# A depthwise convolution of 31 taps on one Trainium2 core, as three short filters on even and odd tokens

## The chip, the cores and the metric

The kernel runs on one core of one Trainium2 chip. The metric is the device time of one execution in microseconds (us), as the median of several runs. The core has five engines with instruction queues of their own: TensorE (PE in the profile, its weight loads PEld), VectorE (DVE), ScalarE (ACT), GpSimd (POOL) and SyncE (SP), which issues most of the DMAs. Each executes its instructions in the order in which they stand in its queue.

## The reference, cut to what matters

The program is a trunk of two layers over 1024 tokens of 1024 features in float32. In each layer the normed input is multiplied by one matrix `w_in`, and its columns are shared by three token mixers: a convolution module (256 channels), differential attention (6 heads) and a gated DeltaNet (6 heads, forward and backward). Their outputs are concatenated, multiplied by `w_out`, and followed by an MLP with a squared ReLU.

The part that the change touches is the convolution module:

```
def conv_module(u, dw_w, dw_b, ln_w, ln_b):
    a, g = jnp.split(u, 2, axis=-1)
    h = a * jax.nn.sigmoid(g)
    h = depthwise_conv(h, dw_w) + dw_b.astype(h.dtype)   # 31 taps, centred, per channel
    h = layer_norm(h, ln_w, ln_b)
    return jax.nn.silu(h)
```

The part that runs beside it is the preparation of the DeltaNet: for each chunk of 64 tokens and each head a unit lower triangular system is solved. The kernel does that by inverting the triangular matrices.

## The kernel before, in words

Per layer there are three stages that follow each other: the input projections (`w_in_phase`), the attention with the DeltaNet scan woven in, and `w_out` with the MLP. The change lies in the first.

**Input projections.** The normed input lies transposed in SBUF as a high and a low part. Blocks of 128 output columns of `w_in` are computed one after the other, each as three products per 128 x 512 block (`mm3`, L163 to L165). For each block the weights are loaded, split on ACT (L168) and DVE (L169), multiplied on PE, and evacuated with what the block needs. The blocks stand in a list `todo`: two blocks of q, k, v for the DeltaNet, the two halves of the convolution's input (`convin`, 128 channels each), five more DeltaNet blocks, then the blocks for attention (`attqk`) and for v and z. `convin` leaves `u`, 128 channels by 1024 tokens with 15 zeros at each end.

**What is woven in.** Between two blocks the loop advances two generators: `prep` by 8 steps and `conv_module` by 6 steps, as soon as both halves of `u` exist. When the list is down to its last 5 entries, both are drained.

```
while todo and len(todo) > self.LATE:
    todo.pop(0)()
    for _ in range(XN):
        next(prep, None)
    if up[1] is not None:
        for _ in range(CN):
            next(conv, None)
```

**conv_module** (L483) works per half `i` on DVE alone: one instruction for the first tap with the bias (L489), then 30 multiply-adds over 1024 tokens (L491), each with the weight of its tap as a scalar per partition, and each reading and writing the accumulator `ca`. Each is followed by a `yield`. Then, in four quarters, PE transposes `ca`, DVE takes mean and variance, POOL the power for the reciprocal root (L158), and PE transposes back.

**prep** goes over three pairs of heads. `dn_a` transposes keys and queries on PE (L652), squares them on ACT (L654), forms decay products on POOL, DVE and ACT (L682 to L686) and the small products of keys and queries on PE (L696). `invert` then inverts the 64 blocks of 32 x 32 of a pair by substitution on POOL: a loop of 31 steps with two instructions each (L765, L766), each depending on the one before:

```
for j in range(B - 1):
    ...
    nc.gpsimd.tensor_tensor(tv, Lp[...], Xm[...], op=ALU.mult)
    nc.gpsimd.tensor_tensor(Xm[:, j + 1:, 0:w], Xm[:, j + 1:, 0:w], tv, op=ALU.subtract)
    yield
nc.scalar.activation(XT, Xm.rearrange("p a b -> p b a"), AF.Copy)
```

The last line (L768) is the transposed copy on ACT; it reads Xm with a step of 32 elements. Ta and Tt are read back from DRAM, two rounds of small products on PE give the 64 x 64 inverses, and they are stored to `kta` (L804). The inversion of a pair runs beside `dn_a` of the next. The DeltaNet scan that follows loads `kta`.

**What sets the order.** The program is written as one stream. A planner simulates it with a cost for each instruction, takes the ready instruction with the earliest place in the stream (or a raised priority, as for the evacuations of the projections), and writes out one fixed order per engine. On the chip an engine waits at its next instruction, even where a later one could go.

Of the kernel before, what the change touches and what calls it, by code (L numbers as in the profile page):

```python
# [9 lines left out]
F32 = mybir.dt.float32  # L10
# [3 lines left out]
ALU = mybir.AluOpType  # L14
# [4 lines left out]
P = 128  # L19
D = 1024  # L20
S = 1024
# [4 lines left out]
TAPS = 31  # L26
# [52 lines left out]
class K:  # L79
# [403 lines left out]
    def conv_module(self, l, L, W, up, dw, db, lw, lb):  # L483
        nc = self.nc
        cas = []
        for i in range(2):
            ca = W.tile([P, S], F32, tag="ca", bufs=2, name=f"ca{l}_{i}")
            u = up[i]
            nc.vector.tensor_scalar(ca, u[:, 0:S], dw[:, i, 0:1], db[:, i:i + 1], ALU.mult, ALU.add)  # L489
            for k in range(1, TAPS):  # L490
                nc.vector.scalar_tensor_tensor(ca, u[:, k:k + S], dw[:, i, k:k + 1], ca, ALU.mult, ALU.add)  # L491
                yield
            cas.append(ca)
        for q in range(4):
            ps = self.bank("sc0", 1).rearrange("p (t k) -> p t k", k=CONV_CH)
            pa = self.bank("sc1", 1).rearrange("p (i t k) -> p i t k", i=2, k=P)
            xc = W.tile([P, 2, CONV_CH], F32, tag="lnx", bufs=2, name=f"lnx{l}_{q}")
            st = W.tile([P, 2, 6], F32, tag="lnst", bufs=2, name=f"lnst{l}_{q}")
            mv = W.tile([P, 2, 2], F32, tag="lnmv", bufs=2, name=f"lnmv{l}_{q}")
            for tt in range(2):  # L500
                t = 2 * q + tt
                for i in range(2):
                    nc.tensor.transpose(ps[:, tt, i * P:(i + 1) * P], cas[i][:, t * P:(t + 1) * P], self.ident)
                nc.vector.bn_stats(st[:, tt], ps[:, tt])
                nc.vector.bn_aggr(mv[:, tt], st[:, tt])
            r = self.rstd(W, mv[:, :, 1], 1.0, 1e-5, "lnr")
            for tt in range(2):
                nc.vector.tensor_scalar(xc[:, tt], ps[:, tt], mv[:, tt, 0:1], r[:, tt:tt + 1], ALU.subtract, ALU.mult)
            yield
            for i in range(2):  # L510
                for tt in range(2):
                    nc.tensor.transpose(pa[:, i, tt], xc[:, tt, i * P:(i + 1) * P], self.ident)
            yo = W.tile([P, 2, CONV_CH], F32, tag="lnx", bufs=2, name=f"yo{l}_{q}")
            for i in range(2):
                nc.scalar.activation(yo[:, i], pa[:, i].rearrange("p t k -> p (t k)"), AF.Silu, scale=lw[:, i:i + 1], bias=lb[:, i:i + 1])
                nc.scalar.dma_start(self.yd[i, :, q * CONV_CH:(q + 1) * CONV_CH], yo[:, i])
            yield
# [1093 lines left out]
```

## Time and profile before

Three runs gave 2972.13, 2974.86 and 2975.39 us, so a median of 2974.86. The profiled execution took 2969.2 us; its span, from the first instruction to the last, is 2967.3.

| engine | busy us | share of the span | instructions |
|---|---|---|---|
| PE | 2730.7 | 92% | 17292 |
| DVE | 2075.6 | 70% | 3701 |
| ACT | 1405.4 | 47% | 2468 |
| POOL | 868.4 | 29% | 793 |

The share is an average over stages that differ. In the chain of work that ended last, PE has 67% of the span and POOL 11%, of which lines 766 and 765 take 4% and 3%; both belong to the input projections. [...]

### The profile page before, as it was taken

Reading aid. Unit: us, or ns where it says so; the run is one execution under the profiler, and the core shown is the slowest. Engines: PE = TensorE matmul, PEld = TensorE weight load, DVE = VectorE, ACT = ScalarE, POOL = GpSimd, SP = SyncE. Lnnn points to the kernel's source line nnn. Section 1 sums busy time; section 2 is a strip of 40 time slices with the busy share of each in tenths; the row PEclk is TensorE's granted clock in tenths of the full one; section 3 lists DMA queues with packets and bytes.
Section 4 is the critical chain, followed back from the end, with each engine's and each line's share of the span. In section 5 each row is a group of like instructions: output and inputs, shape, how many; then the busy total and the mean of one; then the engine's idle time right before and its main releaser. Section 6 shows DMA issues by size and latency. Waiting matters only on the chain.

```text
span 2967.3 us, 46102 instructions
## 1 busy us (share of the span) xinstructions
PE 2730.7 (92%) x17292; PEld 2189.7 (74%) x17292; DVE 2075.6 (70%) x3701; ACT 1405.4 (47%) x2468; POOL 868.4 (29%) x793
## 2 busy tenths in 40 slices
PE   8987979997999998999999689799879999989997
PEld 7865757766888886888787567577658888868886
DVE  5797317888478776777768772378974877767876
ACT  5432315677346665332554223265863566643334
POOL 2288715747000000000112986276550000000000
PEclk9988979998999999999999889799989999999999
DMA  5557785442325557665446487844332355586553
GB/s 136 153 154 207 209 190 148 130 113 81 122 93 196 208 205 295 236 210 188 152 117 141 124 243 198 212 137 122 100 119 81 110 213 200 195 322 244 204 180 117
DMA packets 415312, 504.73 MB, mean 170 GB/s; under 512 B 125401, under 2 KB 313945, under 8 KB 412786
## 3 DMA queue, kind: packets, MB, share of 16 engines
q1 hardware_dynamic: 359362, 373.92, 42.4%
q10 hardware_dynamic: 55728, 127.88, 11.3%
q8 instruction: 136, 2.23, 0.3%
q14 instruction: 86, 0.70, 0.1%
HBM read 318.01 MB, written 182.12 MB: 169 GB/s over the span
## 4 chain that ended last, share of the span: by engine, by line
PE 67%; POOL 11%; DVE 8%; DMA 8%; issue 3%; ACT 2%; SPq 1%; ACTq 0%; DVEq 0%; POOLq 0%
PE at L163 10%; PE at L164 10%; PE at L165 10%; PE sc L163 4%; PE sc L164 4%; PE sc L165 4%; POOL Xm L766 4%; POOL subt L765 3%; DVE sc L1046 2%; PE at L1044 2%; PE dt L163 2%; PE dt L164 2%; PE dt L165 2%; PE tr L1070 2%; PE dt L861 2%
## 5 line engine op out<-in xcount | busy, mean ns | idle before, releaser
L158 POOL TENSOR_TENSOR pro<-pr,mhalf 128x1 f32<-128x1 f32 x32 | 18.5, 578 | 1415.9 <-DVE pr L207 1413.1
L163 PE MATMUL at<-hTh,wh 128*128 128x512 f32 (+1 forms) x832 | 328.4, 396 | 6.7 <-ACT cp L363 6.7
L165 PE MATMUL at<-hTh,wl 128*128 128x512 f32 (+1 forms) x832 | 326.9, 394 | 6.7 <-DVE wl L169 6.7
L164 PE MATMUL at<-hTl,wh 128*128 128x512 f32 (+1 forms) x832 | 327.2, 393 | 0.0
L1049 ACT ACTIVATE sc<-sc,mx 128x1024 f32<-128x1024 f32 x192 | 220.4, 1149 | 85.2 <-DVE mx L1046 82.8
L165 PEld LDWEIGHTS at<-hTh,wl 128*128 128x128 f32 x832 | 160.8, 193 | 39.6 <-DVE wl L169 8.2
L163 PEld LDWEIGHTS at<-hTh,wh 128*128 128x128 f32 x832 | 161.3, 194 | 38.6 <-ACT cp L363 7.5
L164 PEld LDWEIGHTS at<-hTl,wh 128*128 128x128 f32 x832 | 161.2, 194 | 31.1 <-issue 0.7
L491 DVE SCALAR_TENSOR_TENSOR ca<-cu,dw,ca 128x1024 f32<-128x1024 f32 x120 | 171.3, 1443 | 0.4
L1044 PE MATMUL at<-stk 96*128 96x512 f32 x352 | 146.7, 474 | 18.4 <-DVE mx L1046 17.2
L1046 DVE CUSTOM_DVE_ANT_0 sc<-at,bias,mx 128x512 f32<-128x512 f32 x192 | 142.4, 746 | 24.9 <-PE at L1044 19.3
L1046 DVE CUSTOM_DVE_ANT_0 sc<-at,bias 128x512 f32<-128x512 f32 x192 | 130.1, 684 | 37.1 <-PE at L1044 32.0
L765 POOL TENSOR_TENSOR subt<-Lp,Xm 128x31 f32<-128x31 f32 (+15 forms) x186 | 126.6, 680 | 84.1 <-DMA Lp<-ai 50.9
L1156 ACT ACTIVATE ob<-sb 128x512 fp32r<-128x512 f32 x120 | 74.8, 626 | 156.6 <-PE tr L165 49.3
L766 POOL TENSOR_TENSOR Xm<-Xm,subt 128x31 f32<-128x31 f32 (+15 forms) x186 | 144.8, 778 | 13.0
L163 PE MATMUL at<-ob,oa 128*128 128x512 f32 x356 | 138.3, 391 | 2.1 <-ACT at L1484 2.1
L164 PE MATMUL at<-ob,oa 128*128 128x512 f32 x356 | 138.4, 389 | 0.0
L165 PE MATMUL at<-ob,oa 128*128 128x512 f32 x356 | 138.0, 389 | 0.0
L1070 PE MATMUL tr<-consts,sc 128*128 128x128 f32 x704 | 110.4, 289 | 17.3 <-DVE sc L1066 12.2
L1156 ACT ACTIVATE ob<-w2r 128x512 fp32r<-128x512 f32 x92 | 57.5, 628 | 131.6 <-PE tr L165 48.9
L169 DVE TENSOR_TENSOR wl<-wr,wh 128x1024 fp32r<-128x1024 f32 x48 | 64.9, 1353 | 76.2 <-ACT wh L168 76.2
L1074 ACT ACTIVATE aT<-tr 128x512 f32<-128x512 f32 x160 | 91.7, 592 | 39.0 <-PE tr L1070 38.6
(462 smaller groups left out, 7937.5 us busy)
## 6 DMA issues: line engine op xcount, KB each, us to landing
hd<-oa ACTq DMA_DIRECT2D x120, 512.0 KB, 5.7
oa<-hd SPq DMA_DIRECT2D x120, 512.0 KB, 4.2
w1r<-in_w_ff_dram SPq DMA_DIRECT2D x32, 1024.0 KB, 5.6
w2r<-in_w_ff_dram SPq DMA_DIRECT2D x64, 512.0 KB, 7.0
wr<-in_w_in_dram SPq DMA_DIRECT2D x50, 512.0 KB, 5.0
ld<-hd SPq DMA_DIRECT2D x98, 256.0 KB, 4.1
kta<-kta SPq DMA_DIRECT2D x32, 576.0 KB, 8.5
stk<-qk SPq DMA_DIRECT2D x66, 256.0 KB, 4.8
```

The costliest lines, as they stand in the source:

```text
L163: mm(ps, lhsT=lh, rhs=rh, start=first, stop=False, skip_group_check=more)
L164: mm(ps, lhsT=lh, rhs=rl, start=False, stop=False, skip_group_check=more)
L165: mm(ps, lhsT=ll, rhs=rh, start=False, stop=last, skip_group_check=more)
L491: nc.vector.scalar_tensor_tensor(ca, u[:, k:k + S], dw[:, i, k:k + 1], ca, ALU.mult, ALU.add)
L765: nc.gpsimd.tensor_tensor(tv, Lp[:, j + 1:, j:j + 1].broadcast_to([P, n, w]), Xm[:, j:j + 1, 0:w].broadcast_to([P, n, w]), op=ALU.mult)
L766: nc.gpsimd.tensor_tensor(Xm[:, j + 1:, 0:w], Xm[:, j + 1:, 0:w], tv, op=ALU.subtract)
L1044: mm(ps, lhsT=st[:, 0, t * P:(t + 1) * P], rhs=st[:, 1, ks], start=True, stop=True)
L1046: nc.vector.tensor_tensor_reduce(out=sc[:, ks], in0=ps, in1=self.bias[:, o:o + 512], scale=slope, scalar=mx[:, 0:1] if n2 else 3.0e38, op0 ...
L1049: nc.scalar.activation(sc, sc, AF.Exp, scale=-1.0, bias=mx[:, 1:2], accum_out=oS[:, t, mp:mp + 1])
L1070: nc.tensor.transpose(ps[:, k], pp[0][:, (4 * q + k) * P:(4 * q + k + 1) * P], self.ident)
L1074: nc.scalar.activation(aT[:, 4 * q:4 * q + 4, qi * P:qi * P + P], ps, AF.Copy)
L1156: self.nc.scalar.activation(h, src, AF.Copy)
```

## The change

The 31 taps on all tokens become three filters on the even and the odd samples of `u`. With x_e and x_o the even and odd samples, h0 the 16 taps with even number and h1 the 15 with odd number, the output at odd tokens is y_o = (h0+h1) * x_o + h1 * (x_e shifted - x_o), and at even tokens y_e = (h0+h1) * x_o + h0 * (x_e - x_o). The product with h0+h1 is shared. So per half of the channels there are 16 + 16 + 15 instructions over 512 tokens (the first with the bias), two subtractions that form the differences (one in place in `u`, one into a new tile `x1`), and two small instructions that form h0+h1 in a new tile `hs`. Input and output of each are read and written with a step of two elements. A step of the generator is now two taps, and the forming of the differences is a step of its own: 24 steps for a half in place of 30. The new tiles take 2.2 KB per partition in the same pool.

```diff
-            nc.vector.tensor_scalar(ca, u[:, 0:S], dw[:, i, 0:1], db[:, i:i + 1], ALU.mult, ALU.add)
-            for k in range(1, TAPS):
-                nc.vector.scalar_tensor_tensor(ca, u[:, k:k + S], dw[:, i, k:k + 1], ca, ALU.mult, ALU.add)
-                yield
+
+            H, M = S // 2, S // 2 + 15
+            xe, xo = u[:, 0::2], u[:, 1::2]
+            ye, yo = ca[:, 0::2], ca[:, 1::2]
+            h0, h1 = dw[:, i, 0::2], dw[:, i, 1::2]
+            hs = W.tile([P, 16], F32, tag="hs", bufs=2, name=f"hs{l}_{i}")
+            nc.vector.tensor_tensor(hs[:, 0:15], h0[:, 0:15], h1, op=ALU.add)
+            nc.vector.tensor_copy(hs[:, 15:16], h0[:, 15:16])
+            x1 = W.tile([P, M], F32, tag="x1", bufs=1, name=f"x1_{l}_{i}")
+            nc.vector.tensor_tensor(x1[:, 0:M - 1], xe[:, 1:M], xo[:, 0:M - 1], op=ALU.subtract)
+            nc.vector.tensor_tensor(xe, xe, xo, op=ALU.subtract)
+            yield
+            nc.vector.tensor_scalar(yo, xo[:, 0:H], hs[:, 0:1], db[:, i:i + 1], ALU.mult, ALU.add)
+            for k in range(1, 16):
+                nc.vector.scalar_tensor_tensor(yo, xo[:, k:k + H], hs[:, k:k + 1], yo, ALU.mult, ALU.add)
+                if k % 2:
+                    yield
+            nc.vector.scalar_tensor_tensor(ye, xe[:, 0:H], h0[:, 0:1], yo, ALU.mult, ALU.add)
+            for k in range(1, 16):
+                nc.vector.scalar_tensor_tensor(ye, xe[:, k:k + H], h0[:, k:k + 1], ye, ALU.mult, ALU.add)
+                if k % 2:
+                    yield
+            for k in range(15):
+                nc.vector.scalar_tensor_tensor(yo, x1[:, k:k + H], h1[:, k:k + 1], yo, ALU.mult, ALU.add)
+                if k % 2:
+                    yield
```

## Rows read from the trace of the kernel before

**Rows 1.** Layer 0, busy us (instructions) per engine, clock, DMA.

```profile
150.00:235.00 85.00, 58.71 (x271) 46.37 (x269) 67.78 (x76) 27.95 (x33) 73.66 (x72) 0.82 0.51 135
```

**Rows 2.** PE's waits, whole span: us in total, times, longest.

```profile
PE tr L696 <- ACT sq L654: 36.1, 3, 18.0
```

**Rows 3.** PE timeline, layer 0: start, us, instruction, idle before.

```profile
235.89 1.97 PE L696 MATMUL tr<-kq 64*64 64x128 f32 x18 [17.98 <-ACT sq L654]
```

**Rows 4.** ACT timeline, layer 0: the same columns.

```profile
233.41 1.94 ACT L768 ACTIVATE XT<-Xm 128x1024 f32<-128x1024 f32 x1 [16.65 <-POOL Xm L766]
235.25 0.58 ACT L654 ACTIVATE sq<-tr 128x512 f32<-128x512 f32 x1
```

**Rows 5.** Line 765 on POOL, head pairs 0, 1, 2 of layer 0.

```profile
155.00:234.00 79.00, 23.71 (x31) 0.81 0.47 134
244.00:313.00 69.00, 19.48 (x31) 0.98 0.77 231
323.00:367.00 44.00, 18.56 (x31) 0.96 0.64 183
```

**Rows 6.** Line 766 on POOL in the same stretches.

```profile
155.00:234.00 79.00, 30.90 (x31) 0.81 0.47 134
244.00:313.00 69.00, 25.79 (x31) 0.98 0.77 231
323.00:367.00 44.00, 16.76 (x31) 0.96 0.64 183
```

**Rows 7.** POOL timeline, layer 0: start, us, instruction.

```profile
196.70 2.03 POOL L686 TENSOR_TENSOR De<-De,rho 128x512 f32<-128x512 f32 x1
...
206.99 1.55 POOL L766 TENSOR_TENSOR Xm<-Xm,subt 128x255 f32<-128x255 f32 x1
208.61 1.50 POOL L765 TENSOR_TENSOR subt<-Lp,Xm 128x252 f32<-128x252 f32 x1
...
285.08 1.04 POOL L686 TENSOR_TENSOR De<-De,rho 128x512 f32<-128x512 f32 x1
...
339.52 0.64 POOL L765 TENSOR_TENSOR subt<-Lp,Xm 128x252 f32<-128x252 f32 x1
340.24 0.67 POOL L766 TENSOR_TENSOR Xm<-Xm,subt 128x252 f32<-128x252 f32 x1
```

**Rows 8.** DVE timeline, layer 0; a count stands behind x.

```profile
137.86 6.05 DVE L491 SCALAR_TENSOR_TENSOR ca<-cu,dw,ca 128x1024 f32<-128x1024 f32 x5
...
207.93 1.68 DVE L491 SCALAR_TENSOR_TENSOR ca<-cu,dw,ca 128x1024 f32<-128x1024 f32 x1
...
209.54 1.66 DVE L491 SCALAR_TENSOR_TENSOR ca<-cu,dw,ca 128x1024 f32<-128x1024 f32 x1
...
240.65 0.75 DVE L426 SCALAR_TENSOR_TENSOR qkl<-at,consts,qkh 128x512 fp32r<-128x512 f32 x1
241.31 1.28 DVE L491 SCALAR_TENSOR_TENSOR ca<-cu,dw,ca 128x1024 f32<-128x1024 f32 x1
```

**Rows 9.** DVE groups by line, whole span: busy us, mean ns.

```profile
L491 DVE SCALAR_TENSOR_TENSOR ca<-cu,dw,ca 128x1024 f32<-128x1024 f32 x120 | 171.3, 1443 | 0.4
```

**Rows 10.** ACT groups by line, whole span.

```profile
L168 ACT ACTIVATE wh<-wr 128x1024 fp32r<-128x1024 f32 x50 | 52.9, 1058 | 56.3 <-PE at L164 52.2 <-issue 1.6 <-DMA wr<-in_w_in_dram 1.6
...
L768 ACT ACTIVATE XT<-Xm 128x1024 f32<-128x1024 f32 x6 | 12.1, 2014 | 59.5 <-POOL Xm L766 59.5
```

**Rows 11.** Line 491 on DVE in three stretches of layer 0.

```profile
104.00:137.50 33.50, 17.58 (x12) 1.00 0.43 126
156.00:224.00 68.00, 28.39 (x19) 0.86 0.53 151
244.00:297.00 53.00, 23.11 (x16) 0.97 0.80 234
```

**Rows 12.** Chain of work that ended last, 366 to 440 us.

```profile
373.64 3.87 DMA Ta<-xi
...
396.65 8.02 DMA kta<-kta
```

## The prediction

> **What bounds the kernel now.** I read the busy table first: TensorE (PE) is busy 92% of the span, so the time moves only where PE is left waiting or where the chain runs through something else. The convolution runs only in two stretches, one per layer, so next I asked for the busy time of layer 0's stretch. From 150 to 235 us GpSimd (POOL) is busy 73.66 of 85 us, VectorE (DVE) 67.78, PE only 58.71, and PE's granted clock averages 0.82 [rows 1]. The view of PE's waits says what that hole is: of 36.1 us at line 696 the longest wait is 18.0 [rows 2]; the timeline shows it end at 235.89 [rows 3]. The other half of the 36.1 is its twin in layer 1.
>
> The releaser named there, the square at line 654, is a proxy. In ScalarE's (ACT) timeline that square starts right behind the activation that writes XT (L768), which sat for 16.65 us until POOL's last update of Xm [rows 4]. ACT works in order, so everything PE needs from it stood behind the end of the block inversion on POOL (L765 and L766, 62 dependent instructions per head pair). The end of that loop is what PE waits for.
>
> Then: why is the loop slow? Its last run, for head pair 2, is the measure of an almost undisturbed one: 18.56 + 16.76 = 35.3 us of work. Pair 0 needed 23.71 + 30.90 = 54.6, pair 1 19.48 + 25.79 = 45.3 [rows 5, 6]. POOL's timeline shows how: two steps at 339.52 and 340.24 lie 0.72 us apart, two of about the same size at 206.99 and 208.61 lie 1.6 apart, each instruction itself stretched to 1.5 [rows 7]. The decay products (L686) grow from 1.04 to 2.03 in the same way [rows 7]. In DVE's timeline two taps of the convolution start at 207.93 and 209.54, also 1.61 apart, where five undisturbed ones together take 6.05, 1.20 each [rows 8]. So where both engines have work of this kind they take turns: one DVE instruction, one POOL instruction, and POOL waits about 1.6 - 0.72 = 0.88 us per turn. That wait, not DVE's busy time, is what the convolution costs the critical path.
>
> **The change, part by part.** *Arithmetic on DVE.* Per half of the channels, before: 31 taps at 1.20 start to start [rows 8], the first, which has no second tensor, counted like the others: 37.2 us. With the turns the mean of 120 taps is 1.443 [rows 9]. After: 47 taps on 512 columns, two subtractions of 526 and 527 columns, and two operations on 15 and 1 columns. The row nearest to a 512-column multiply-add with a per-partition factor is L426: one starts at 240.65, the next instruction at 241.31, 0.66 [rows 8]. So 47 x 0.66 = 31.0; the subtractions 2 x 0.66 = 1.3; the small two 0.3 (an estimate: above nothing, at most 0.66 each). Sum 32.6, a saving of 4.6 per half, 18 us over four halves. The saving is that small because half the columns cost 0.66 and not 0.60. I count none of it directly: DVE is not what PE waits for at 235.
>
> [...]
>
> *Stride.* Every operand now takes every second float. No row shows DVE at that stride. Below it, the dense 0.66. Above it, the nearest are ACT's: XT reads Xm 32 floats apart and takes 2014 ns against 1058 for a dense copy of 1024 [rows 10], 1.9 times. I take the dense price, since eight bytes is nearer to dense than to 128, and keep 1.9 as a rival. [...] By ACT's row alone the sum would be the stride rival below.
>
> *POOL's turns.* A tap of half the length keeps POOL waiting 0.54 less (1.20 - 0.66): 0.88 becomes 0.34. There are 47/31 = 1.52 times as many taps to meet. For pair 0 the loop's excess is 54.6 - 35.3 = 19.3, and L686 and L682 inside it some 4 more [rows 5 to 7], 23 us or 26 turns. The convolution has 19 taps in 156 to 224 and 28.39 us of DVE time [rows 11]; the other DVE instructions with two SBUF inputs there (L169, L370, L371, L683) are as many but partly shorter, so I give it 0.6 of the turns (0.5 to 0.8): 16 turns, 14.1 us. After: 16 x 1.52 = 24.3 turns of 0.34, 8.3. Pair 0 ends 5.8 us sooner (3 to 8). Pair 1: 10.0 + 3 = 13 us, 15 turns, 9 of them (16 taps, 23.11 us [rows 11]): 7.9 becomes 4.7, 3.2 sooner. Pair 2 runs when the convolution is over: nothing.
>
> *What PE gets.* The 18.0 us hole shrinks by pair 0's 5.8; ACT and the square have nothing else to wait for. The late part of the stretch hangs on pair 2's end, since Ta lands from 373.64 and the kta transfer starts at 396.65 [rows 12]; between them PE's dense products stand. So the tail moves by between 5.8 and 5.8 + 3.2 = 9.0; I take 7 per layer.
>
> *Start of the loop.* Pair 0 starts when A is stored, behind 12 taps that DVE does from 104 to 137.5 [rows 11]. Each step of the generator issued one tap of 1.20; now it issues two halves, 1.32, after a first step of 1.6 without any tap. For the same 12 steps that is 1.6 + 11 x 1.32 = 16.1 against 12 x 1.20 = 14.4, but fewer columns are then left to do; I cost it at 0.5 per layer (-2 to +3, since the order is found anew).
>
> *Program order.* The two halves need 48 generator steps in place of 60. At six per projection the LayerNorm comes two projections sooner. Its transposes and POOL's rstd move into pair 1's time; they were not late before, so I cost this at nothing. If that cover is gone, it costs POOL four instructions of 0.7 per layer, 3 us.
>
> *Sum.* (7 - 0.5) x 2 = 13 us. The profiled execution takes 2969.2 (span 2967.3 and 1.9 around it), so 2956; the median of the runs is 2974.86, 5.7 above it, so 2962.
>
> **Rivals.** (1) *Nothing arrives (within 6 us).* PE's tail is set by its own dense products and by the loads behind kta, or POOL simply meets a half tap at every step: 62 steps x 0.34 = 21 against 19.3 now. For: DVE is 80% busy there, so more steps can be met [rows 1]. Against: the taps are finite, 19 become 29. Time 2975.
>
> (2) *Stride price, slower.* Place: all 47 taps. At 1.9 times the column time a tap takes 0.12 + 1.9 x 0.54 = 1.15 and 47 of them 54, 17 us more per half. POOL's wait is back at 0.88 - 0.05 with 1.52 times as many turns: 24.3 x 0.83 = 20 against 14.1, and 13.7 x 0.83 = 11.4 against 7.9, 9.5 later per layer; the steps ahead of the loop become 1.6 + 22 x 1.15 = 26.9 and add 12. (9.5 + 12) x 2 = 43: 3018. It decides from where a half tap costs more than about 0.85. Against: eight bytes is far from 128.
>
> (3) *Another order on ACT, either sign.* Each engine's order is written out from a simulated timeline. If one more evacuation that PE needs falls behind pair 1's XT, PE gets a second hole of up to 15 us per layer: 2962 + 30 = 2992. If line 654's square falls ahead of pair 0's XT, the two holes, 36.1 together [rows 2], largely close, and the gain is that and little more: about 2938. Nothing in the profile favours either.
>
> **How the numbers follow.** A measurement of this kernel tells about 0.2%, 6 us, from no change. Chances: forecast 0.45 (2950 to 2968), nothing arrives 0.22, stride 0.1, other order against 0.15, for 0.08. Faster: 0.45 + 0.08 and less a part of the forecast's own range, 0.53; same 0.21; slower 0.26. The range goes from 2938 to 2990: it leaves out the stride case and the ends of the order cases.
>
> **What would show it.** Right: taps at 0.72 to 0.78 us; POOL's contended steps near 1.06 apart in place of 1.6; L765 and L766 together near 49 for pair 0 and 42 for pair 1; the wait at L696 near 12. Wrong: taps above 0.85 (stride), the pair sums unchanged (turns met twice as often), or the wait at L696 unchanged while the sums fell (something else stands before it on ACT). It fails as a whole if PE's busy time or the parts of the trace without convolution move by more than a few us.

## The result, and the profile after

The changed kernel takes 2935.28 us (median of 4 runs, 2934.27 to 2939.61) against 2974.62 for the kernel before on the same chip: a ratio of 0.9873, 95% interval 0.9858 to 0.9889. That is 39 us faster where 13 were forecast, and below the low end of the range. The profiled execution has a span of 2933.3 us against 2967.3.

From here on "the kernel before" has the line numbers above; in the changed kernel lines behind the convolution are 22 higher (765 and 766 become 787 and 788, XT's 768 becomes 790, the square's 654 becomes 676), and the taps are lines 503, 508 and 512.

The same 85 us of layer 0 as in [rows 1], in the changed kernel; the columns are length, busy us and count for PE, PEld, DVE, ACT and POOL, granted clock (the share of full speed that PE was given, 0.955 over the whole execution before and 0.964 after), DMA share, GB/s:

```profile
150.00:235.00 85.00, 64.98 (x320) 51.41 (x318) 71.93 (x101) 30.70 (x36) 75.20 (x76) 0.90 0.59 155
```

PE does 320 products there in place of 271, at a clock of 0.90 in place of 0.82. The view of PE's waits for the whole span (total, times, longest) shows that the wait on the square [rows 2] is all but gone (2.2 us in total, where 36.1 stood) and that smaller ones stand in its place:

```profile
PE dt L811 <- DMA Ta<-xi: 15.4, 5, 8.3
...
PE tr L718 <- DVE Aqk L723: 12.1, 4, 5.0
...
PE sc L525 <- DVE ca L512: 8.3, 2, 7.3
PE at L163 <- DVE qkl L426: 8.1, 1, 8.1
...
PE tr L718 <- ACT sq L676: 2.2, 3, 0.9
```

ScalarE's timeline (start, duration, instruction, idle before) says why: in the order that was found anew, the square stands 18 us ahead of XT and no longer behind it [rows 4]. What stands behind XT now is the evacuation of line 425, hence the 8.1 us at line 163.

```profile
209.09 0.60 ACT L676 ACTIVATE sq<-tr 128x512 f32<-128x512 f32 x1 [1.27 <-DVE ssk L677]
...
227.72 1.98 ACT L790 ACTIVATE XT<-Xm 128x1024 f32<-128x1024 f32 x1 [15.42 <-POOL Xm L788]
229.59 0.69 ACT L425 ACTIVATE qkh<-at,consts 128x512 fp32r<-128x512 f32 x1
```

XT itself starts at 227.72 against 233.41 in [rows 4], 5.7 us sooner. The steps of the loop, line 787 and then line 788, for head pairs 0, 1 and 2 (compare [rows 5, 6]):

```profile
155.00:228.00 73.00, 23.41 (x31) 0.93 0.51 152
238.00:296.50 58.50, 22.02 (x31) 0.91 0.81 235
306.00:349.50 43.50, 16.52 (x31) 1.00 0.76 220
```

```profile
155.00:228.00 73.00, 26.98 (x31) 0.93 0.51 152
238.00:296.50 58.50, 22.50 (x31) 0.91 0.81 235
306.00:349.50 43.50, 18.55 (x31) 1.00 0.76 220
```

The sums are 50.4, 44.5 and 35.1 us, where 54.6, 45.3 and 35.3 stood before and 49 and 42 were forecast for the first two. So pair 1's sum hardly fell in layer 0; in layer 1 it is 41.8 after 46.3. POOL's timeline shows contended steps 1.05 to 1.09 apart, in place of 1.6 [rows 7]:

```profile
201.89 0.98 POOL L787 TENSOR_TENSOR subt<-Lp,Xm 128x255 f32<-128x255 f32 x1
202.95 1.01 POOL L788 TENSOR_TENSOR Xm<-Xm,subt 128x255 f32<-128x255 f32 x1
204.04 0.97 POOL L787 TENSOR_TENSOR subt<-Lp,Xm 128x252 f32<-128x252 f32 x1
205.09 1.02 POOL L788 TENSOR_TENSOR Xm<-Xm,subt 128x252 f32<-128x252 f32 x1
```

DVE's timeline has the other side of it: three taps undisturbed, 0.66 apart, and three in the contended place, 1.05 to 1.09 apart:

```profile
140.22 0.74 DVE L512 SCALAR_TENSOR_TENSOR ca<-x,dw,ca 128x512 f32<-128x512 f32 x1
140.88 0.74 DVE L508 SCALAR_TENSOR_TENSOR ca<-cu,dw,ca 128x512 f32<-128x512 f32 x1
141.54 0.74 DVE L503 SCALAR_TENSOR_TENSOR ca<-cu,hs,ca 128x512 f32<-128x512 f32 x1
...
202.29 1.13 DVE L512 SCALAR_TENSOR_TENSOR ca<-x,dw,ca 128x512 f32<-128x512 f32 x1
203.34 1.17 DVE L508 SCALAR_TENSOR_TENSOR ca<-cu,dw,ca 128x512 f32<-128x512 f32 x1
204.43 1.12 DVE L503 SCALAR_TENSOR_TENSOR ca<-cu,hs,ca 128x512 f32<-128x512 f32 x1
```

A single turn is as long as forecast, yet the gain is three times as large. To see where it lies, I cut the span into stages: the input stage of a layer, up to the first transpose of vtE (line 973 before), and the attention behind it, up to its last product with V (line 1079 before). The second layer begins with its first gate product (line 352). The kernel before, columns as above:

```profile
0.00:433.90 433.90, 362.32 (x2623) 290.56 (x2623) 244.74 (x363) 153.25 (x210) 232.04 (x262) 0.92 0.64 174
433.90:730.50 296.60, 277.46 (x2747) 205.44 (x2748) 246.97 (x619) 201.33 (x388) 186.83 (x112) 0.94 0.41 113
1487.40:1906.90 419.50, 358.34 (x2597) 288.59 (x2595) 243.41 (x356) 144.28 (x198) 222.50 (x254) 0.90 0.63 169
1906.90:2205.60 298.70, 273.43 (x2748) 201.70 (x2748) 252.37 (x619) 202.37 (x388) 189.98 (x112) 0.96 0.41 113
```

The changed kernel:

```profile
0.00:410.30 410.30, 358.86 (x2622) 287.36 (x2622) 243.72 (x404) 154.95 (x211) 221.89 (x262) 0.95 0.66 182
410.30:718.60 308.30, 282.82 (x2749) 208.55 (x2749) 247.36 (x617) 204.55 (x389) 189.95 (x112) 0.93 0.40 112
1473.70:1877.30 403.60, 352.04 (x2597) 283.49 (x2596) 237.53 (x396) 142.14 (x195) 213.58 (x254) 0.92 0.64 176
1877.30:2171.20 293.90, 273.77 (x2747) 200.65 (x2748) 248.17 (x619) 200.28 (x388) 186.78 (x112) 0.97 0.41 114
```

Both input stages together are 853.4 us before and 813.9 after: 39.5 sooner. Of it 29.7 is time in which PE did nothing (length less busy time: 132.7 becomes 103.0), 9.8 is the same products done faster, at a clock of 0.95 and 0.92 in place of 0.92 and 0.90. Attention is 6.9 us longer in this execution: PE is busy 5.7 us longer with the same products there and idle 1.2 us longer. Over the kernels below it lies between 591 and 616 us, so it tells little of the change. The input stages tell more, with one exception below (XT on GpSimd). Every experiment below has their sum beside its time; it comes from one profiled execution each. The ratios come from all runs, against runs of the kernel before on the same chip (medians of 2972.9 to 2974.6), and decide where the two differ.

### The profile page after: what moved, and what is told of

Read it like the earlier page. It is cut to its first block, busy times and chain, and to the rows that moved or that the text cites. A ratio compares the mean times of both kernels' runs of the same rounds, so it can differ in the third digit from the quotient of the medians.

```text
span 2933.3 us, 46208 instructions
## 1 busy us (share of the span) xinstructions
PE 2727.2 (93%) x17292; PEld 2183.9 (74%) x17292; DVE 2064.8 (70%) x3781; ACT 1406.6 (48%) x2468; POOL 850.3 (29%) x793
## 4 chain that ended last, share of the span: by engine, by line
PE 65%; POOL 11%; DMA 9%; DVE 7%; issue 4%; ACT 3%; SPq 1%; ACTq 0%; DVEq 0%; POOLq 0%
PE at L163 10%; PE at L164 10%; PE at L165 10%; POOL Xm L788 4%; PE sc L163 4%; PE sc L164 4%; PE sc L165 4%; POOL subt L787 4%; PE dt L163 2%; PE dt L164 2%; PE dt L165 2%; DVE sc L1068 2%; PE at L1066 2%; PE tr L1092 2%; DMA qkT<-gq 2%
## 5 line engine op out<-in xcount | busy, mean ns | idle before, releaser
L1066 PE MATMUL at<-stk 96*128 96x512 f32 x352 | 149.0, 478 | 17.4 <-DVE mx L1068 15.9
L1068 DVE CUSTOM_DVE_ANT_0 sc<-at,bias 128x512 f32<-128x512 f32 x192 | 129.9, 684 | 40.5 <-PE at L1066 31.1
L1178 ACT ACTIVATE ob<-sb 128x512 fp32r<-128x512 f32 x120 | 74.8, 626 | 155.1 <-PE tr L165 54.8
L788 POOL TENSOR_TENSOR Xm<-Xm,subt 128x31 f32<-128x31 f32 (+15 forms) x186 | 132.9, 714 | 12.9
L1092 PE MATMUL tr<-consts,sc 128*128 128x128 f32 x704 | 111.8, 289 | 14.8 <-DVE sc L1088 6.2
L1086 POOL TENSOR_TENSOR sc<-sc,sc 128x1024 f32<-128x1024 f32 x40 | 104.8, 2623 | 21.2 <-ACT sc L1083 20.5
```

The lines of the kernel that those rows point to most:

```text
L1066: mm(ps, lhsT=st[:, 0, t * P:(t + 1) * P], rhs=st[:, 1, ks], start=True, stop=True)
L1068: nc.vector.tensor_tensor_reduce(out=sc[:, ks], in0=ps, in1=self.bias[:, o:o + 512], scale=slope, scalar=mx[:, 0:1] if n2 else 3.0e38, op0 ...
L1086: self.lastpool = nc.gpsimd.tensor_tensor(pp[0], pp[0], pp[1], op=ALU.add)
L1092: nc.tensor.transpose(ps[:, k], pp[0][:, (4 * q + k) * P:(4 * q + k + 1) * P], self.ident)
L1178: self.nc.scalar.activation(h, src, AF.Copy)
```

## The experiments

Two things change with the taps: the instructions on DVE, and the written-out order of all engines, which is found anew. Theory 1 gives the taps the 13 us of the forecast and the order the rest. Theory 2 makes the order a bystander. In most kernels below the order of every engine is held to that of one of the two kernels, by an order-only dependency of each instruction on the one written before it; the taps themselves are left free among DVE's other instructions, except where it is said:

```diff
+    for e, seq in ORDER_OF_THE_KERNEL_BEFORE.items():
+        for last, i in zip(seq, seq[1:]):
+            tc.add_manual_dep(i, last.name, nosync, reason="order")
```

**Taps and order apart.** *Short taps in the old order* (the diff above, with the new convolution in 30 steps):

> The changed kernel's filters of 16, 16 and 15 taps, while the order of all instructions that are not the convolution's is held, on every engine, to that of the kernel before (30 steps per half, as before). Theory 1 (the shorter DVE instructions give about 13 us, and the rest of the 39 us comes from the engines' order, which was found anew): 2958 to 2966 us, with the wait of PE on the square at the end of the inversion still there, about 12 us per layer. Theory 2 (the order is a bystander, the cheaper convolution gives it all): 2932 to 2940. Theory 3 (the cheaper convolution gives nothing in the old order): 2972 to 2977.

Measured 2951.63, ratio 0.9926 (0.9912 to 0.9939): 22 us faster, input stages 828.7. More than theory 1 allowed and less than theory 2 asked. Its four stages:

```profile
0.00:419.60 419.60, 359.09 (x2624) 288.39 (x2624) 239.22 (x405) 153.84 (x211) 217.03 (x262) 0.94 0.65 180
419.60:719.40 299.80, 281.87 (x2748) 208.25 (x2748) 246.07 (x617) 201.90 (x388) 186.78 (x112) 0.93 0.40 112
1474.40:1883.50 409.10, 357.27 (x2597) 287.44 (x2595) 239.17 (x396) 144.83 (x197) 208.32 (x254) 0.91 0.64 174
1883.50:2189.40 305.90, 282.64 (x2747) 208.69 (x2748) 251.19 (x619) 203.22 (x388) 190.03 (x112) 0.93 0.39 110
```

POOL's busy time in the input stages falls by 15.0 and 14.2 us, and the stages by 14.3 and 10.4. PE's wait on the square (line 725 here) is still there, and as long as forecast, 12.7 against 18.0:

```profile
PE tr L725 <- ACT sq L683: 26.4, 3, 12.7
```

*Full taps in the new order* (the diff above with the order of the changed kernel, and the old convolution in 24 steps):

> The kernel before's 31 taps on all 1024 columns, while the order of all other instructions is held, on every engine, to that of the changed kernel (24 steps per half). Theory 1 (order gives about 26 us by itself): 2945 to 2953, with no wait of PE on the square behind XT. Theory 2 (the order gives nothing by itself): 2972 to 2978, or more, as this order was made for shorter taps.

Measured 2972.93, ratio 0.9999 (0.9985 to 1.0012); input stages 847.9. So the order gives nothing clear of noise with full taps; in the profiled execution layer 0's input stage is 10.0 us shorter than before and layer 1's 4.6 longer. The taps give 22 us in the old order and 39 in the new: the two parts don't add, and theory 1 in its plain form is false.

**The square's place.** *Before, with pair 0's XT behind the squares* (every engine's order held, this one swap on ACT; XT_0 is pair 0's XT, sq_2_1_0 and sq_2_1_1 are the last squares of head pair 2):

```diff
  order of ACT, layer 0:   ... XT_0, sq_2_1_1 ...            -> ... sq_2_1_1, XT_0 ...
  order of ACT, layer 1:   ... XT_0, sq_2_1_0, sq_2_1_1 ...  -> ... sq_2_1_0, sq_2_1_1, XT_0 ...
```

> The kernel before, every engine's order held, with one swap in ScalarE's: pair 0's XT goes behind the squares of head pair 2 that stood right behind it (one in layer 0, two in layer 1). Theory 1a (the place of the squares is the whole of the order's part): 2943 to 2953, the waits of 18.0 and 16.7 us on the square gone. Theory 1b (the hole only moves to the next evacuation that stands behind XT, and the gain needs the rest of the new order): 2965 to 2974. Theory 2: 2972 to 2977.

Measured 2971.4, ratio 1.0005 (0.999 to 1.002); input stages 855.6. The two waits of 18.0 and 16.7 us on the square are gone from PE's waits, and no gain is seen: by the interval it is 3 us at most. The next evacuation behind XT takes their place (line 170 here is 163):

```profile
PE at L170 <- DVE qkl L433: 20.2, 3, 12.9
```

*The changed kernel, with the squares right behind XT* (the reverse of that swap):

> The changed kernel, every engine's order held, with the squares of head pair 2 moved from ahead of pair 0's XT to right behind it (the last one in layer 0, the last two in layer 1), as the kernel before has them. Theory 1a: back to 2956 to 2966, with two waits on the square of about 12 us each. Theory 1b (other parts of the order matter more): 2938 to 2950. Theory 2: 2933 to 2938.

Measured 2943.6, ratio 0.9905 (0.9889 to 0.9921), 8 us of the 39 lost; input stages 825.2, 11.3 longer. The wait on the square is back at 20.6 us at its longest:

```profile
PE tr L725 <- ACT sq L683: 36.7, 2, 20.6
```

*Short taps, old order, squares ahead of XT* (both edits above together):

> Short taps in the order of the kernel before, with the one swap on ScalarE: pair 0's XT behind the squares of head pair 2. That swap was worth nothing with full taps (ratio 1.0005), its reverse cost the changed kernel 8 us. Theory P (the square's place pays only once the loops on GpSimd end sooner): 2940 to 2946. Theory Q (it pays only with the rest of the new order): 2949 to 2954, with PE's wait moved from the square to the evacuation of line 425 behind XT.

Measured 2954.0, ratio 0.9935 (0.9922 to 0.9947); input stages 832.1 against 828.7 without the swap. Theory Q: of the runs here, the square's place is worth something only inside the new order.

**What in the taps gives the 22 us.** *Each full tap as two dense halves, at the same place of DVE's order* (62 short instructions per half of the channels, every order held, the taps' too):

```diff
-  scalar_tensor_tensor(ca, u[:, k:k + S], dw[:, i, k:k + 1], ca, MULT, ADD)
+  for a in (0, S // 2):
+      scalar_tensor_tensor(ca[:, a:a + S // 2], u[:, a + k:a + k + S // 2], dw[:, i, k:k + 1], ca[:, a:a + S // 2], MULT, ADD)
```

> The kernel before with each of the 31 taps issued as two instructions of 512 adjacent columns, at the same place of DVE's order, and every other instruction's order held. No arithmetic is saved: 62 short taps per half where the changed kernel has 47. Theory A (what counts is the length of the instruction that GpSimd waits for): the loops of pair 0 and 1 still end sooner, 5 us per layer together by the prediction's 0.34 us per turn; the start of pair 0's loop may come up to 7 us later: 2962 to 2976, and pair 0's loop is shorter than 77.8 us. Theory B (what counts is DVE's time in the convolution): 62 x 0.79 = 49 against 31 x 1.28 = 39.7 us per half, slower: 2985 to 3010, and pair 0's loop longer.

Measured 2963.16, ratio 0.9969 (0.9953 to 0.9985): 9 us faster, input stages 845.5, although DVE has more to do. Theory A: a shorter instruction alone helps GpSimd. Undisturbed, these dense halves start as far apart as the strided taps of the changed kernel, (6.70 - 0.74) / 9 = 0.66 us:

```profile
140.00 6.70 DVE L506 SCALAR_TENSOR_TENSOR ca<-cu,dw,ca 128x512 f32<-128x512 f32 x10
```

Pair 0's loop takes 75.0 us from its first step to XT, where 77.8 stood, but starts 3.4 us later. The other 17 us of input stage between this kernel and the short taps in the old order (845.5 to 828.7) come with 49 long operations per half in place of 62. Of these, 5.4 lie ahead of the loops: with 62, pair 0's first step comes 3.9 us later in layer 0 and 1.5 in layer 1. (In the kernel with 49 the taps' places on DVE were free as well, so a part of the 17 may be theirs.)

*The first tap alone, in the old order and in the new:*

```diff
-  for k in range(1, TAPS):
-      scalar_tensor_tensor(ca, u[:, k:k + S], dw[:, i, k:k + 1], ca, MULT, ADD)
```

> The kernel before with the first tap alone in each half (120 of 124 taps left out), every other instruction's order held: what the whole convolution costs in that order. Prediction's working: pair 0's loop loses its 19 + 4 us of excess, pair 1's its 10 + 3, so 36 us per layer at POOL; PE's hole of 18 closes and the tail follows as far as PE's dense products let it: 2900 to 2925. If the changed kernel in the old order (2952) already has most of that, 2940 to 2950.

> The first tap alone in each half (120 of 124 taps left out) in the changed kernel's order; in the old order it took 2916. The new order gave 0 with full taps and 16 with short ones. If it gains the more the less the convolution holds GpSimd up: 2896 to 2904. If it is fitted to the short taps: 2910 to 2920.

Measured 2916.12, ratio 0.981 (0.9788 to 0.9831), input stages 792.7, and 2902.99, ratio 0.9759 (0.9746 to 0.9772), input stages 776.8. All but the first tap of each half costs 56 us in the old order, and the short taps give back 22 of these. The new order gives 13 us here. So it is not fitted to the short taps: it pays with little convolution and not with the full one. The wait on the square is 12.9 us even here, in the old order; what one wait of PE measures is not what its cause costs.

**Is it the pace, or one lucky order?**

```diff
  x5: the 51 operations of the new convolution over 30 steps per half, order found anew
  x6: the 31 full taps over 24 steps per half, order found anew
```

> The changed kernel with the 51 operations of a half spread over 30 steps of the generator, as before, in place of 24; the order of all engines is found anew. If the new order's 16 us beside the short taps are typical of what is found around short taps: 2928 to 2942. If they hang on this one order: anywhere from 2945 to 2965.

> The kernel before's 31 taps in 24 steps of the generator in place of 30, order found anew. The prediction costs the faster pace at nothing: 2969 to 2980. If the pace makes the gain: 2940 to 2960.

Measured 2939.5, ratio 0.9885 (0.9862 to 0.9909), input stages 821.7; and 2975.35, ratio 1.0008 (0.9996 to 1.0019), input stages 852.9. The pace is worth nothing, as forecast. A second order found around short taps gains 12 us over the old order (7 of input stage), where the first gained 16 (15 of input stage); the interval of the second, some 7 us to either side, does not tell them apart.

**Which part of the new order.** In the old order POOL interrupts pair 1's loop for the two powers of head pair 2. POOL's timeline of the short taps in the old order has them behind the third step:

```profile
242.45 3.36 POOL L699 TENSOR_TENSOR rkinv<-sse,phalf 128x16 f32<-128x16 f32 x1
245.78 3.36 POOL L699 TENSOR_TENSOR rq<-sse,mhalf 128x16 f32<-128x16 f32 x1
```

In the new order they run ahead of that loop, in a time in which POOL had waited. They need the squares, so this would join the square's place to POOL's chain (theory R). *The three moves together, in the old order, with short and with full taps; and the powers alone moved back, in the new order:*

```diff
  ACT:  squares of head pair 2 ahead of XT_0 (as above)
  DVE:  sse (line 662) right behind the last reduction of the squares (line 655)
  POOL: rkinv, rq of pair 2 (line 670) right behind pair 0's last step of line 766
```

> Short taps in the order of the kernel before (2951.6; with the square swapped 2954.0), with one chain moved together: the last squares of head pair 2 ahead of pair 0's XT on ScalarE, the sum sse right behind their reduction on VectorE, and GpSimd's two powers for pair 2 (rkinv and rq, 3.36 us each) right behind pair 0's last step, into the time in which it waits, instead of behind the third step of pair 1's loop. Theory R (this is what the new order gives: 6.7 us off GpSimd's chain per layer): 2936 to 2944, pair 1's loop without its interruption. Theory S (the gain lies elsewhere in the new order): 2949 to 2956.

> The same three moves in the kernel before with its full taps. Theory R by GpSimd's chain alone: 6.7 us per layer here too, 2958 to 2964. What the whole new order did with full taps (ratio 0.9999): 2971 to 2977.

> The changed kernel, every engine's order held, with GpSimd's two powers for head pair 2 moved back behind the third step of pair 1's loop in both layers; the squares stay where they are. Theory R: 2943 to 2950. Theory S: 2933 to 2939.

Measured 2952.51 (ratio 0.9938, 0.9915 to 0.9961), 2970.25 (0.9994, 0.998 to 1.0008) and 2938.9 (0.9889, 0.9865 to 0.9913); input stages 828.8, 854.4 and 816.4. Theory R falls in the first two. The third does not decide: its interval, 2933 to 2947 us, covers theory S and more than half of R. POOL's timeline of the first shows that pair 1's loop has no powers in it any more. Yet from its first step to XT it takes 58.7 us, where 60.1 stood with 6.7 of powers in it. A part of the difference is that POOL now waits for two loads of R inside it, 1.06 + 2.84 = 3.9 us, as these stand where they stood (the 4.44 lie ahead of the first step, where 5.74 were idle without the moves). And the loop begins 2.8 us later, as pair 0's ended 2.2 later in this execution:

```profile
229.17 2.90 POOL L699 TENSOR_TENSOR rkinv<-sse,phalf 128x16 f32<-128x16 f32 x1
232.03 2.90 POOL L699 TENSOR_TENSOR rq<-sse,mhalf 128x16 f32<-128x16 f32 x1
...
240.49 1.06 POOL L711 TENSOR_TENSOR R<-R,gc 128x512 f32<-128x512 f32 x1 [4.44 <-DMA R<-cr]
...
250.48 1.06 POOL L711 TENSOR_TENSOR R<-R,gc 128x512 f32<-128x512 f32 x1 [1.06 <-DMA R<-cr]
...
255.75 1.22 POOL L711 TENSOR_TENSOR R<-R,gc 128x512 f32<-128x512 f32 x1 [2.84 <-DMA R<-cr]
```

The third kernel has a hint of why the powers' place matters so little: with the powers back in it, the loop of pair 1 spends 39.0 us in its steps in place of 44.5 (40.5 in place of 41.8 in layer 1). Of the 30 operations of the convolution beside pair 1, 18 overlap a step in place of 26; others run beside the powers and stretch no step. DVE's timeline of short taps in the old order shows two of them beside the first power above, at the undisturbed 0.74:

```profile
243.17 0.74 DVE L514 SCALAR_TENSOR_TENSOR ca<-cu,dw,ca 128x512 f32<-128x512 f32 x1
243.83 0.74 DVE L516 SCALAR_TENSOR_TENSOR ca<-x,dw,ca 128x512 f32<-128x512 f32 x1
```

*One engine held to the old order, the others found anew around the short taps:*

```diff
-    for e, seq in ORDER_OF_THE_KERNEL_BEFORE.items():
+    for e, seq in {"PE": ...}.items():       # e2
+    for e, seq in {"POOL": ...}.items():     # e3
```

> Short taps, TensorE's order alone held to that of the kernel before; the four other engines' orders are found anew. With all five orders old it took 2952, with all five new 2935 (24 steps) and 2940 (30 steps). If TensorE's order carries the 12 to 16 us: 2949 to 2955. If TensorE only follows: 2934 to 2942.

> Short taps, GpSimd's order alone held to that of the kernel before; the four other engines' orders are found anew. If GpSimd's order carries the 12 to 16 us: 2949 to 2955. If not: 2934 to 2942.

Measured 2952.06 (ratio 0.9926, 0.991 to 0.9941) and 2958.63 (0.9953, 0.9938 to 0.9967); input stages 829.8 and 828.0. In sum the old order on either engine takes the whole of the new order's gain. By layers it is less plain: with PE's old order layer 1's input stage is 403.6 us, as in the changed kernel, and layer 0's 426.2, longer than with all orders old (419.6); with POOL's they are 405.7 and 422.3. Also, the other engines' orders were found anew around the held one, so these are two orders more, not the new one with one part put back. That the gain is a property of the orders together fits these runs, but they do not show it.

**Other versions.** Three tries to go below the changed kernel, all with its convolution:

```diff
  w2: order of ACT: XT_0 behind the next evacuation of line 425
  w1: -  nc.scalar.activation(XT, Xm.rearrange("p a b -> p b a"), AF.Copy)
      +  nc.gpsimd.tensor_copy(XT, Xm.rearrange("p a b -> p b a"))
  p4: -  rkinv, rq = pow(sse, +0.5), pow(sse, -0.5) on GpSimd
      +  rt = sqrt(sse) on ScalarE; rkinv = copy(rt[:, 0]), rq = reciprocal(rt[:, 1]) on VectorE
```

> The changed kernel, every engine's order held, with pair 0's XT moved on ScalarE behind the next evacuation of line 425 in both layers, whose second stage PE waited for 8.1 us in layer 0. If PE's waits at this place are on the path: 2925 to 2932. If the stage's end hangs on GpSimd's chain and the wait is only moved work: 2932 to 2941.

> The changed kernel with XT written by GpSimd, right behind its own loop, in place of ScalarE; order found anew. ScalarE no longer stands 13 to 16 us behind the loop, GpSimd gets one more instruction per pair on its chain (about 2 us by ScalarE's duration). If ScalarE's standing still costs PE what the two waits of 8 us say: 2922 to 2932. If GpSimd's chain sets the stage's end: 2936 to 2948.

> The changed kernel with the two powers of each head pair (6.7 us of GpSimd per pair, 20 per layer) replaced by one square root on ScalarE, a copy and a reciprocal on VectorE; order found anew. If GpSimd's chain sets the end of the input stage: two of three pairs' powers are on it, at least 6.7 us per layer and up to 13: 2908 to 2925. If it does not: 2930 to 2940, and the added table loads on ScalarE (1.28 us each, 7 more) may show.

Measured 2939.01 (ratio 0.9882, 0.9866 to 0.9899), 2936.66 (0.9874, 0.9858 to 0.9889) and 2948.05 (0.9918, 0.9893 to 0.9943); input stages 817.1, 828.7 and 804.1. None is faster than the changed kernel. In the first, PE's wait on line 426 in layer 0 stays at 8.0 us: one more evacuation went ahead of XT and the next one behind it is waited for. In the second, one wait on Ta of 14.5 us stands in layer 0, where that evacuation's had been. Its input stages are 14.8 us longer than the changed kernel's and its attention, 591 us, is the shortest of all, at the same time for the whole: here the input stages alone would mislead. The third is the instructive miss: 20 us of powers per layer leave POOL, yet POOL's busy time falls by only 14 to 15 per layer, and the input stages by 9.8 in sum. Attention is the longest of all, 615.9, in that execution; in layer 1 PE is busy 289 us there in place of 274, at a granted clock of 0.93 in place of 0.97.

## Why the prediction was wrong

The direction was right; the size was not: 39 us in place of 13. Two terms of the sum failed: pair 1's turns, at 3.2 us per layer, and the order of the engines, at nothing. The input stages of the profiled executions divide the gain like this: 853.4 with full taps, 845.5 with taps of half length alone, 828.7 with the new convolution, 813.9 with the new order on top. The ratios agree: 9, 13 and 16 us for the three steps. ScalarE's timeline shows where along the chain it arrives. XT (here of head pair 1, then 2, in layer 0) starts as soon as a pair's loop has ended; the kernel before, short taps in the old order, and the changed kernel:

```profile
312.34 1.97 ACT L768 ACTIVATE XT<-Xm 128x1024 f32<-128x1024 f32 x1 [8.55 <-POOL Xm L766]
366.36 2.15 ACT L768 ACTIVATE XT<-Xm 128x1024 f32<-128x1024 f32 x1 [6.19 <-POOL Xm L766]
...
298.86 2.13 ACT L797 ACTIVATE XT<-Xm 128x1024 f32<-128x1024 f32 x1 [4.46 <-POOL Xm L795]
355.36 2.13 ACT L797 ACTIVATE XT<-Xm 128x1024 f32<-128x1024 f32 x1 [6.21 <-POOL Xm L795]
...
296.01 2.12 ACT L790 ACTIVATE XT<-Xm 128x1024 f32<-128x1024 f32 x1 [7.29 <-POOL Xm L788]
348.89 2.13 ACT L790 ACTIVATE XT<-Xm 128x1024 f32<-128x1024 f32 x1 [4.14 <-POOL Xm L788]
```

So much sooner than in the kernel before, in us from the layer's beginning (layer 0, then layer 1):

| | XT of pair 0 | XT of pair 1 | XT of pair 2 | end of the input stage |
|---|---|---|---|---|
| forecast, each layer | 5.3 | 8.5 | 8.5 | 6.5 |
| short taps, old order | 6.4, 5.0 | 13.5, 13.8 | 11.0, 11.1 | 14.3, 10.4 |
| changed kernel | 5.7, 5.0 | 16.3, 16.9 | 17.5, 15.3 | 23.6, 15.9 |

(The forecast's row is 5.8 and 5.8 + 3.2 less 0.5 for the start, and its 7 less 0.5.) Pair 0 came as forecast, pair 1 brought twice as much and more, and what the new order adds comes behind pair 0.

*The size of a turn, and the stride: right.* Steps 1.05 to 1.09 apart were forecast as 1.06; undisturbed taps take 0.74 and start 0.66 apart, the dense price of line 426 [rows 8]. The stride rival is out. (Its 0.12 us per instruction is an estimate from [rows 8]: the 0.66 of 512 columns less the 0.54 that the other 512 add.) Near enough were the start of pair 0's loop (forecast 0.5 later; first step at 155.6 as before, with short taps in the old order at 155.1) and pair 0's share: from its first step to XT the loop took 77.8 us and takes 71.9 with short taps in the old order, 5.9 less (4.3 in layer 1), against 5.8.

*Pair 1's share: mis-sized.* The forecast was 3.2 per layer. Measured in the same way, with the order held, 67.5 becomes 60.1 and in layer 1 68.7 becomes 60.7: 7.4 and 8.0. The step that failed is the number of turns: 9 before, and "There are 47/31 = 1.52 times as many taps to meet". While pair 1 is dealt with (XT of pair 0 to XT of pair 1), DVE did 19 full taps in the kernel before and does 26 short operations. Counted in the timelines of DVE and POOL, 14 of the 19 overlap a step of the loop and 16 of the 26 (13 and 14 in layer 1): 1.1 times as many, not 1.52. The others run beside the powers or while POOL waits. At the forecast's own 0.88 and 0.34 us per turn, 14 and 16 turns are 12.3 and 5.4 us, so 6.9 less (6.7 in layer 1), close to the 7.4 and 8.0. The same count for pair 0 is 14 and 25 (16 and 26), so 3.8 and 5.2 less; there 1.6 to 1.8 times as many were met (forecast: 16 and 24.3). This is an estimate made after the fact: it counts overlaps, not waits. In the changed kernel pair 1 can't be read alone, as the two powers stand ahead of its loop there: 57.2 and 57.8 us, and 6 us of powers outside.

*"I take 7 per layer": too little, and the number of instructions.* With the order held both shares, 13.3 and 12.3 us as measured, reached the end of the stage nearly whole: 14.3 and 10.4 us per layer, where I had 6.5. The number of DVE's instructions weighed more than the forecast gave it: dense halves, undisturbed 0.66 us apart like these, give 8 us of input stage; taking their number from 62 to 49 per half goes with 17 more, where the forecast's own working has 4 per layer, 8 in all, for 47 taps in place of 62. DVE's busy time does not show it: 120 taps took 171.3 us [rows 9], 180 of the short ones take 165.3, contention included, and with the first taps and the subtractions DVE is about as busy with the convolution as before. (Columns: busy us, mean ns, idle before.)

```profile
L512 DVE SCALAR_TENSOR_TENSOR ca<-x,dw,ca 128x512 f32<-128x512 f32 x60 | 57.5, 958 | 0.0
L508 DVE SCALAR_TENSOR_TENSOR ca<-cu,dw,ca 128x512 f32<-128x512 f32 x60 | 54.6, 911 | 0.1
L503 DVE SCALAR_TENSOR_TENSOR ca<-cu,hs,ca 128x512 f32<-128x512 f32 x60 | 53.2, 887 | 0.4
```

What fell is POOL's busy time, 232.0 to 217.0 in the first input stage with the order held. While the order is held, its fall goes with the stage's: 15.0 and 14.2 us against 14.3 and 10.4 for short taps, 6.9 and 5.9 against 3.5 and 4.4 for dense halves, 34.7 and 28.5 against 33.0 and 27.6 for the first tap alone. With the order found anew it does not: 10.1 and 8.9 against 23.6 and 15.9. More DVE instructions do not lose by their number alone in this place: 62 short taps per half beat 31 long ones by the ratio of 0.9969, and pair 0's loop on POOL, which runs beside them, takes 75.0 us in place of 77.8.

*"What PE gets": the wrong measure.* I read PE's wait at line 696 as the price of the loop. With the order held it shrank from 18.0 to 12.7, as forecast, while the stage shrank by 14.3. With the swap on ACT it vanished and the time stayed. It was a symptom that moves along the order; the end of the input stage goes with pair 2's loop. In the twenty kernels here it comes 60 to 70 us behind that loop's last step in layer 0 (64 to 69 in layer 1), while the step itself lies anywhere from 324 to 367 us.

*Rival 3, the order: its number came true, its mechanism did not.* The square did go ahead of pair 0's XT and the time came near the 2938 of that rival. But the rival said that closing the two holes is the gain. Closing them alone gave nothing, twice. The new order gave 0 with full taps, 16 with short ones, 13 with one. So the sum should have had a term for an order found anew around a lighter convolution; I costed it as chance, at nothing on the mean, and it gave 16 of the 39 us. (In the chances, 0.53 for faster is 0.45 + 0.08 with nothing taken off, though the text says that a part is.)

*The last sign was none.* The parts without convolution were not to move by more than a few us. Attention moved by 6.9, but over the kernels here it moves by 25, so this tells nothing of the mechanism.

*Open:* which combination of places makes the new order better, and why it is worth nothing with full taps. In the old order neither the square's place alone nor the square, its sum and the powers moved together gave it, and the pace did not either. Putting the squares back in the new order cost 8 of its 16 us. With PE's or POOL's old order held, no order with the gain was found. Whole orders of two or three engines held together were not tried. Nor was a kernel with 49 short operations whose places on DVE are held, which would divide the 17 us between number and places.

## What to carry to other kernels

Where two engines take turns, price the change by the busy time of the engine that is on the chain, with both the length and the number of the other's instructions, and count for each stage of the chain, in the two timelines, how many of them it really meets. The longest wait of the bounding engine, with a named releaser, is not the gain to be had: move that one instruction in the existing order and see whether the stage's end moves. And when a planner writes all engines' orders, hold the order once and free it once: here the two gave 22 and 0 us apart and 39 together.

## What the runs showed of the hardware

Reading and writing every second float cost DVE nothing: 0.74 us for 512 columns of a multiply-add, 0.66 from start to start, as for the dense halves of the same taps.

GpSimd's power is dear by the element: 128x16 takes 2.90 to 3.36 us where a subtraction of 128x512 takes 1.06 to 1.22, in the fences on the powers.

PE's time in attention was longest where its clock was lowest, though no instruction had changed there. The same 2747 or 2748 products of layer 1's attention took PE 273.43, 282.64 and 273.77 us in the three kernels of the stage tables, at a granted clock of 0.96, 0.93 and 0.97. What the clock lacks to 1, times the stage's length, is 12, 21 and 9 us of full-speed time not granted, an estimate from these rows; it is enough for the 9 us of difference.
